# Soft mixture of experts by block sums on one core: ScalarE in program order, the first weight piece in two transfers, some z made later, the last round's stores on another queue

## The chip, the core and the metric

The kernel runs on one core of a Trainium2 chip. A core has five engines, each with its own instruction queue: TensorE (PE in the profile) multiplies matrices, VectorE (DVE) and ScalarE (ACT) work on elements and empty PSUM, GpSimd (POOL) and SyncE (SP) issue DMA transfers here. Weights, activations and intermediate blocks lie in SBUF; the results of matmuls lie in PSUM, which has eight banks of 128 x 512 float32 numbers. The metric is the device time of one execution, in microseconds (us).

## The reference

```python
batch, seq, hidden, n_experts, expert_hidden = 16, 512, 512, 8, 2048
...
probs = softmax(router_logits)               # over the 8 experts
for e in range(n_experts):
    expert_out = np.matmul(x, expert_weights[e])
    output += probs[:, :, e:e+1] * expert_out
```

(The softmax is written out there as exp of the logits less their maximum, divided by its sum.) There are 8192 rows of x. For one row, the output is a single long product: the row times each of its eight probabilities, all eight side by side (8 x 512 = 4096 numbers), times the eight weight matrices on top of each other (4096 x 2048). The kernel calls the left factor z.

## The kernel before

The long product is done in halves: two halves of the 8 experts (4 each), two halves of the 2048 columns, and 256-row blocks of x taken in pairs. On this 2 x 2 x 2 structure a Strassen-Winograd scheme is used, seven block products in place of eight, made of sums of z blocks, sums of weight blocks and sums of result blocks. The names a11, s1 to s4, t1 to t4, m1 to m7 in the code are those of that scheme. Inside most block products the same scheme is used once more. Matmuls take float16 operands and add up in float32.

The stages, in order of time:

1. *The start* (lines 196 to 439). `cast_x` and `cast_w` load x rows and weight pieces on GpSimd's queue, with a cast to float16; a weight piece is one expert's 512 rows by 512 columns, 512 KB in SBUF, and two pieces fill one `w` tile. The softmax of the first rows is computed, and the z of rows 0 to 511 is made by TensorE itself: x times a diagonal matrix of probabilities (`diag`, `early_z0`), evacuated from PSUM to SBUF by VectorE and ScalarE in turn (`evacuate`). Then the first product is made plainly, for two column halves n: four experts, four groups j of 128 rows, four chunks c of 128 hidden numbers, with one PSUM bank for each j (loop at 415 to 438). Four ScalarE copies (L432) empty those banks, and SyncE stores them. Behind each column half, `early_z1` makes the z of two of the groups j = 4 to 7 (rows 512 to 1023 of this order), 16 matmuls of 256 columns a time, two matmuls to a bank, for the next stage. The weight sums of the inner scheme (`inner_weights`, four VectorE instructions on a whole `w` tile each) are made between the two halves.
2. *Four stages of inner Strassen products* (`sub_product`, called for r = 1, 5, 2 and 4). Each result block goes to DRAM: `kept1`, `kept5`, `kept2`, and for r = 4 straight into the output. A generator (`prep`) loads and sums the next stage's weights meanwhile.
3. *The last stage* (line 578 on), 16 rounds q, each for one pair of row blocks. A round works on four quarters (row group t, column half n). For each quarter it loads the kept blocks m1, m5 and m2 (`load_kept`, `c11`); ScalarE copies m1 from SBUF into a PSUM bank (L604), and TensorE adds 16 matmuls to it (`plain` with w6). Such a copy into a bank that matmuls are then added to is called a *seed* here. VectorE reads the bank plus m5 into v, TensorE adds another 16 matmuls (w7) into the same bank, ScalarE copies it out (c21, L620), GpSimd adds it to the output in DRAM, VectorE sums it with m5 once more. Then, in round 0, four plain products with w3 follow, seeded with v (L637); in the later rounds an inner Strassen product of seven (`prod`): number 1 is copied to r1 (L666), number 2 is added to a bank seeded with v00 (L653), number 7 leaves a bank that ScalarE copies to r3 (L677) and that VectorE then sums in `put(2, ...)`; number 4 goes to a bank seeded with -v10, and its sum with r3 (`o10`) is made at the start of the next round.

VectorE prepares the z blocks of the next round between these sums (`a11`, `s2`, `s3`, `s4`, called by `ahead`); `early` loads the next round's first kept blocks and makes m1 + m2 (`c11`) and has GpSimd store it.

What sets the order. The program is written as one stream, and a scheduler places each instruction in its engine's queue from its own estimate of times, among those that it takes to be ready. `tc.keep_in_program_order(i)` ties an instruction behind the one traced before it on its engine. The helper `dve` does this for every VectorE instruction while `pinned[0]` is set, which it is in the start and in the last stage:

```python
    def dve(i):
        note(i)
        if pinned[0]:
            tc.keep_in_program_order(i)
```

ScalarE's copies have no such tie in the kernel before: `nc.scalar.copy(x, rows.m1[tn])` at L604 can stand in ScalarE's queue ahead of the copies that the text has before it. An engine takes its queue in order, so an instruction that waits holds all behind it. A tile's buffer is used again when its last reader is done (`m` has 5 buffers, `v` 4, `u` 4, `r` 2 in the last stage); PSUM's eight banks go round the same way.

Of the kernel before, what the change touches and what calls it, by code (L numbers as in the profile page):

```python
# [32 lines left out]
def kernel(  # L33
# [77 lines left out]
    def note(i):  # L111
        last[i.ins.engine] = i.ins

    def dve(i):
        note(i)
        if pinned[0]:
            tc.keep_in_program_order(i)

    def tt(o, a, b, op):
        dve(nc.vector.tensor_tensor(out=o, in0=a, in1=b, op=op))  # L120

# [11 lines left out]
    def pool(o, i):  # L133
        note(nc.gpsimd.dma_start(out=o, in_=i))  # L134

    def bank():
        return psum.tile([P, NB], f32, name="ps", tag="ps")

    def mm(ps, z, w, start, stop):
        nc.tensor.matmul(ps, z, w, start=start, stop=stop, skip_group_check=True)  # L140
# [5 lines left out]
    def new_w():  # L146
        return wpool.tile([P, K8, NB], f16, name="w", tag="w")

    def cast_w(q, kn, e, t):
        k, n = kn  # L150
        pool(t[:, ds(e * C, C), :],
             expert_weights[(q // 10 - 1) * HE + 2 * k + e, :,
                            ds((q % 10 - 1) * NH + n * NB, NB)].rearrange("(c p) n -> p c n", p=P))

    def load(what, kn, gate=True):
        t = new_w()
# [10 lines left out]
        stored[what, kn] = d = dram.tile([P, K8, NB], f16, name=f"wd{what}_{kn[0]}{kn[1]}")  # L167
        sp(d, t)

    def inner_weights(b, t3=None):  # L170
        t1 = new_w()
        tt(t1, b[0, 1], b[0, 0], SUB)
        yield
        t2 = new_w()
        tt(t2, b[1, 1], t1, SUB)
        t4 = new_w()
        tt(t4, t2, b[1, 0], SUB)
        yield
        t3 = t3 or b[0, 1]
        tt(t3, b[1, 1], b[0, 1], SUB)  # L180
        return {1: b[0, 0], 2: b[1, 0], 3: b[1, 1], 4: t4, 5: t1, 6: t2, 7: t3}


    def softmax(lg, J):
# [33 lines left out]
    with behind():  # L218
        for kn in BLOCKS[:3]:
            for e in range(2):  # L220
                cast_w(11, kn, e, b11[kn])
    cast_x(4)
    cast_x(6)
    for e in range(2):
# [13 lines left out]

    def evacuate(o, ps, i):
        if i % 2:  # L240
            note(nc.scalar.copy(o, ps))  # L241
        else:
            dve(nc.vector.tensor_copy(o, ps))  # L243

# [17 lines left out]
    def diag_j(j):  # L262
        return diag(ph0[1][:, :, ds(j % 4, 1)])

    def early_z1(j, d):
        for k in range(2):
            for c in range(0, C, 2):
                ps = bank()
                for i in range(2):
                    mm(ps[:, ds(i * 2 * P, 2 * P)], xs0[:, j, ds((c + i) * P, P)],  # L270
                       d[:, ds(2 * k, 2)].rearrange("p e t -> p (e t)"), i == 0, i == 1)
                evacuate(z1[j // 2 - 2][k][:, :, ds(c, 2), ds(j % 2 * P, P)],
                         ps.rearrange("p (c e t) -> p e c t", c=2, e=2), c // 2)


    R = 4
# [66 lines left out]
        sp(t, kept[r][i][n, ds(u * P, P), :])  # L343
        return t

    def sub_product(r, odd, first, w, prep, start=0, zs=None):

        for d in range(start, NI // 2):
            if zs:
# [13 lines left out]
            s2 = new(s1, a11, SUB)  # L363
            s4 = new(a12, s2, SUB)
            tt(a21, a11, a21, SUB)
            z = {1: a11, 2: a12, 3: s4, 4: a22, 5: s1, 6: s2, 7: a21}

            for u in range(HQ // P):
# [46 lines left out]
    for n in range(2):  # L415
        ps = [bank() for _ in range(4)]
        for e in range(HE):
            if n == 0 and e < HE - 1:
                if e < 2:
                    ds_.append(diag_e(e + 2))  # L420
                early_z0(e + 1, ds_[e + 1])
            for j in range(4):
                for c in range(C):
                    mm(ps[j], z0[j][:, e, c], b11[e // 2, n][:, e % 2 * C + c, :],
                       e + c == 0, e == HE - 1 and c == C - 1)
        if n == 0:
            ph0.append(early_p(1))
            ds_ = [diag_j(j) for j in range(4, 6)]
            softmax_of_all()
        for j in range(4):  # L430
            o = half()
            nc.scalar.copy(o, ps[j])  # L432
            to_kept(1, j // 2, j % 2, n, o)
        for i in range(2):
            early_z1(4 + 2 * n + i, ds_[i])
        if n == 0:
            ds_ = [diag_j(j) for j in range(6, 8)]
            with behind():
                w = finish(inner_weights(b11, new_w()))

    def weights_of_t1():
        b = {}
        for i, kn in enumerate(BLOCKS):
# [6 lines left out]
    pinned[0] = False  # L450
    share(xs=3, r=4, o=8)
    sub_product(1, 0, P1, w, weights_of_t1(), 1,
                [[z.rearrange("p e c t -> p (e c) t") for z in zz] for zz in z1])


    def weights_of_21():
# [50 lines left out]
    class Rows:  # L507
# [55 lines left out]
            self.put(0, 0, tn, m2)  # L563

        def put(self, odd, cols, tn, o, **how):
            nc.gpsimd.dma_start(out=out_rows(self.q, odd, tn[0], cols, tn[1]), in_=o, **how)  # L566

    rows = Rows(0)
    for make in (rows.a11, rows.s2, rows.s3):
# [8 lines left out]
    for q in range(NI):  # L578
# [11 lines left out]


        xs, vs = [], []
        if o10:
            o10()
        for j, tn in enumerate(QUARTERS):
            if j > 1:
                rows.load_kept(j)
                rows.c11(j)
            if j < 2:
                rows.s4(j)  # L600
            else:
                ahead("a11", j - 2)
            x = bank()
            nc.scalar.copy(x, rows.m1[tn])  # L604
            plain(x, 6, w6, tn, False)
            v = half("u")
            tt(v, x, rows.m5[tn], ADD)
            xs.append(x)
            vs.append(v)


        if q == 1:
# [3 lines left out]
        for j, tn in enumerate(QUARTERS):  # L616
            x, m5 = xs[j], rows.m5[tn]
            plain(x, 7, w7, tn, False)
            c21 = half("m")
            nc.scalar.copy(c21, x)  # L620
            rows.put(1, 0, tn, c21, accum_op=ADD)
            tt(m5, x, m5, ADD)
            rows.put(1, 1, tn, m5)
            if j < 2:
                ahead("s2", j)


        def early(j):
            if following:
                following.load_kept(j)  # L630
                following.c11(j)

        ahead("s3", 0)
        if q == 0:
            for j, tn in enumerate(QUARTERS):
                y = bank()
                nc.scalar.copy(y, vs[j])  # L637
                plain(y, 3, w3, tn, False)
                nc.scalar.copy(vs[j], y)
                rows.put(0, 1, tn, vs[j])  # L640
                if j < 2:
                    early(j)
                    next(sums)
            ahead("s3", 1)
            rows = following
            continue
        banks = {}

        def prod(p, b, seed=None, scale=1.0):
            if b not in banks:  # L650
                banks[b] = bank()
                if seed is not None:
                    nc.scalar.mul(banks[b], seed, scale)  # L653
            for k in range(K8):
                mm(banks[b], z3[p][:, k, :], inner3[p][:, k, :],
                   p in (1, 5) and k == 0, k == K8 - 1)
            return banks[b]
# [5 lines left out]
        v00, v01, v11, v10 = vs  # L663
        x = prod(1, "x")
        r1 = half("r")
        nc.scalar.copy(r1, x)  # L666
        put(0, prod(2, "b", v00), r1, ADD)
        early(0)
        r5 = prod(5, "q")
        tt(v11, r5, v11, ADD)  # L670
# [3 lines left out]
        put(1, prod(3, "q"), v01, ADD)  # L674
        prod(7, "x")
        r3 = half("r")
        nc.scalar.copy(r3, x)  # L677
        put(2, x, v11, ADD)
        ahead("s3", 1)
        d = prod(4, "d", v10, -1.0)  # L680

        def o10(put=put, r3=r3, d=d):
            put(3, r3, d, SUB)
# [30 lines left out]
```

## Time and profile before

| | us |
|---|---|
| median of 3 runs (lowest to highest) | 1446.75 (1442.5 to 1447.27) |
| the profiled execution's own time | 1446.23 |
| its span, first to last instruction | 1444.5 |
| TensorE busy | 1427.5 (99%) |
| VectorE busy | 1021.1 (71%) |
| ScalarE busy | 270.8 (19%) |
| GpSimd busy | 228.8 (16%) |
| granted TensorE clock | 0.998 of full speed |

The profile is of one execution. A line such as "L120 DVE TENSOR_TENSOR h<-ps,h" is an instruction of VectorE, written at line 120 (here a helper, `tt`), that reads the tiles ps and h and writes an h. In a timeline, the bracket at the end tells how long the engine stood idle before the first instruction of the line and what ended the wait. "PE" is a matmul, "PEld" the load of its stationary operand. Matmuls overlap in their pipeline, and their ends are modelled, so the length of one (379 ns in the mean) is longer than the step from one to the next. DMA transfers that a queue issues are listed with the queue (SPq, POOLq) and their time from issue to landing.

### The profile page before, as it was taken

To read this page: it belongs to the slowest core of one execution; us is meant where nothing else is said; L and a number is where in the kernel's file an instruction comes from. 1 tells how busy PE (TensorE), PEld (TensorE's weight loads), DVE (VectorE), ACT (ScalarE), POOL (GpSimd) and SP (SyncE) were. 2 spreads that over 40 slices of the span, in tenths; PEclk is the share of its full clock that TensorE was granted. 3 is DMA by queue.
4 is the path that set the end of the run, shared out by engine and by line. 5 is a ranking of instruction groups with operands and counts; after the bars stand their busy time and mean duration, and the time that the engine had idled before them with its cause. 6 is when DMAs were issued, how large, how long until landed. Compare 5 with 4: busy or idle time off the path is not lost.

```text
span 1444.5 us, 18192 instructions
## 1 busy us (share of the span) xinstructions
PE 1427.5 (99%) x6661; PEld 649.3 (45%) x6661; DVE 1021.1 (71%) x1171; ACT 270.8 (19%) x475; POOL 228.8 (16%) x357
## 2 busy tenths in 40 slices
PE   8999999999999999999999999999999999999997
PEld 4444444444444444444444444444444444444443
DVE  6857686747686867766757496777778787776774
ACT  3211111111111111111112111111111111111111
POOL 3100100110001000001000122222222222222222
PEclk9999999999999999999999999999999999999999
DMA  9989968899839994368866976787787777777773
GB/s 192 206 199 258 263 175 188 191 243 272 216 134 310 348 354 151 131 190 225 212 248 221 277 203 207 228 232 233 234 232 221 211 216 223 218 231 218 226 204 102
DMA packets 194073, 319.44 MB, mean 221 GB/s; under 512 B 54080, under 2 KB 83776, under 8 KB 189376
## 3 DMA queue, kind: packets, MB, share of 16 engines
q1 hardware_dynamic: 135616, 199.77, 44.8%
q0 software_dynamic: 58368, 118.51, 34.2%
q8 instruction: 52, 0.85, 0.2%
q14 instruction: 37, 0.30, 0.1%
HBM read 180.65 MB, written 159.58 MB: 236 GB/s over the span
## 4 chain that ended last, share of the span: by engine, by line
PE 52%; issue 34%; POOL 11%; DMA 1%; DVE 1%; POOLq 0%; ACT 0%; DVEq 0%; SPq 0%
PE ps L140 52%; POOL out_dram L566 11%; DMA w<-in_expert_weights_dram 1%; DVE h L120 0%; POOLq L566 0%; POOL w L134 0%; DMA out_dram<-h 0%; DMA h<-kept 0%; DVE z L120 0%; DVE z L243 0%; ACT h L432 0%; DVE h L190 0%; DVE h L191 0%; DVE h L186 0%; ACT h L188 0%
## 5 line engine op out<-in xcount | busy, mean ns | idle before, releaser
L140 PE MATMUL ps<-w,z 128*128 128x512 f16 x6552 | 1415.7, 379 | 5.2 <-DVE h L120 3.3
L140 PEld LDWEIGHTS <-z 128*128 128x128 f16 x6552 | 640.8, 98 | 778.3 <-issue 5.0
L120 DVE TENSOR_TENSOR h<-ps,h 128x512 f32<-128x512 f32 x389 | 265.7, 686 | 266.6 <-PE ps L140 65.8
L120 DVE TENSOR_TENSOR z<-xT,pT 128x2048 f16<-128x2048 f16 x248 | 299.3, 1218 | 31.9 <-PE ps L140 31.9
L120 DVE TENSOR_TENSOR z<-z 128x2048 f16<-128x2048 f16 x280 | 303.6, 1107 | 7.8 <-DVE z L120 0.5
L380 ACT COPY h<-ps 128x512 f32<-128x512 f32 x248 | 145.4, 586 | 601.6 <-PE ps L140 598.3
L566 POOL DMA_DIRECT2D out_dram<-h x256 | 162.1, 660 | 540.6 <-DVE h L120 499.9
L120 DVE TENSOR_TENSOR h<-h 128x512 f32<-128x512 f32 (+1 forms) x67 | 46.0, 686 | 78.7 <-DMA h<-kept 78.6
L620 ACT COPY h<-ps 128x512 f32<-128x512 f32 x64 | 37.5, 586 | 294.3 <-PE ps L140 208.6
L120 DVE TENSOR_TENSOR w<-w 128x4096 f16<-128x4096 f16 x36 | 82.2, 2286 | 3.3 <-DMA w<-wdt 2.0
L604 ACT COPY ps<-h 128x512 f32<-128x512 f32 x64 | 37.5, 588 | 197.9 <-DMA h<-kept 197.9
L134 POOL DMA_DIRECT2D h<-in_x_dram x32 | 22.5, 703 | 283.8 <-DMA xT<-h 249.9
L120 DVE TENSOR_TENSOR h<-h,ps 128x512 f32<-128x512 f32 x77 | 52.5, 682 | 11.6 <-PE ps L140 11.3
L134 POOL DMA_DIRECT2D w<-in_expert_weights_dram x40 | 29.9, 759 | 173.3 <-issue 77.3
L134 POOL DMA_DIRECT2D w<-wd x12 | 6.5, 543 | 188.3 <-DVE w L158 115.2
L653 ACT ACTIVATE ps<-h 128x512 f32<-128x512 f32 x30 | 18.2, 607 | 0.0
L243 DVE CAST z<-ps 128x512 f16<-128x512 f32 x16 | 10.2, 684 | 10.5 <-PE ps L140 10.5
L666 ACT COPY h<-ps 128x512 f32<-128x512 f32 x15 | 8.8, 586 | 16.4 <-PE ps L140 16.4
L241 ACT CAST z<-ps 128x512 f16<-128x512 f32 x16 | 8.4, 601 | 11.9 <-PE ps L140 11.9
L140 PE MATMUL ps<-h,w 128*128 128x128 f16 (+1 forms) x96 | 8.2, 237 | 2.3 <-DMA w<-in_x_dram 1.0
L677 ACT COPY h<-ps 128x512 f32<-128x512 f32 x15 | 8.7, 580 | 7.6 <-PE ps L140 7.6
L140 PEld LDWEIGHTS <-w 128*128 128x128 f16 x96 | 6.9, 98 | 4.3 <-DMA w<-in_x_dram 2.2
(31 smaller groups left out, 38.3 us busy)
## 6 DMA issues: line engine op xcount, KB each, us to landing
out_dram<-h POOLq DMA_DIRECT2D x256, 256.0 KB, 4.6
kept<-h SPq DMA_DIRECT2D x192, 256.0 KB, 4.7
h<-kept SPq DMA_DIRECT2D x192, 256.0 KB, 4.3
pT<-p_dram SPq DMA_DIRECT2D x124, 256.0 KB, 4.8
w<-in_expert_weights_dram POOLq DMA_DIRECT2D x40, 512.0 KB, 12.4
out_dram<-h SPq DMA_DIRECT2D x64, 256.0 KB, 3.7
xT<-x SPq DMA_DIRECT2D x60, 256.0 KB, 2.8
w<-wd POOLq DMA_DIRECT2D x12, 1024.0 KB, 9.4
```

Of the source, the lines that this page charges most:

```text
L120: dve(nc.vector.tensor_tensor(out=o, in0=a, in1=b, op=op))
L134: note(nc.gpsimd.dma_start(out=o, in_=i))
L140: nc.tensor.matmul(ps, z, w, start=start, stop=stop, skip_group_check=True)
L241: note(nc.scalar.copy(o, ps))
L243: dve(nc.vector.tensor_copy(o, ps))
L380: nc.scalar.copy(t, ps)
L566: nc.gpsimd.dma_start(out=out_rows(self.q, odd, tn[0], cols, tn[1]), in_=o, **how)
L604: nc.scalar.copy(x, rows.m1[tn])
L620: nc.scalar.copy(c21, x)
L653: nc.scalar.mul(banks[b], seed, scale)
L666: nc.scalar.copy(r1, x)
L677: nc.scalar.copy(r3, x)
```

## The change

- A second helper, `act`, is the same function as `dve`. The ScalarE copies of `evacuate`, of the first product's banks and of the whole last stage go through it, so they stay in program order in the start and in the last stage.
- In the last stage the seed of a quarter's bank now stands ahead of `o10` and of the quarter's `c11` in the text; the seeds of the banks "b" and "d" (in round 0 those of the first two w3 products) are written right behind the four w6 products, and the other two of round 0 behind the first two w3 products. The fourth copy and store of round 0 moves to the next round's `o10`. `c11` of round 1's first two quarters moves from round 0 into round 1.
- `cast_w` can load one expert's piece in two transfers of 256 KB (hidden chunks 0 and 1, then 2 and 3); this is used for the very first piece. In the first product the chunk loop c is now outside the group loop j.
- `early_z1` takes one (j, k) at a time, 8 matmuls, and all eight calls move into the second column half's product: two behind expert 0, three behind expert 1, three behind expert 2. The inner weight sums (`inner_sums` returns them as four callables) are made one behind expert 1, one behind the product, and two inside the first `sub_product`, after its z sums.
- In the last round (q = 15) the stores to the output that do not accumulate are issued by SyncE in place of GpSimd.

```diff
+    act = dve
...
-    def cast_w(q, kn, e, t):
+    def cast_w(q, kn, e, t, parts=1):
         k, n = kn
-        pool(t[:, ds(e * C, C), :],
-             expert_weights[(q // 10 - 1) * HE + 2 * k + e, :,
-                            ds((q % 10 - 1) * NH + n * NB, NB)].rearrange("(c p) n -> p c n", p=P))
+        for c in range(0, C, C // parts):
+            pool(t[:, ds(e * C + c, C // parts), :],
+                 expert_weights[(q // 10 - 1) * HE + 2 * k + e, ds(c * P, C * P // parts),
+                                ds((q % 10 - 1) * NH + n * NB, NB)].rearrange("(c p) n -> p c n", p=P))
...
+    def inner_sums(b, t3=None):
+        t3 = t3 or b[0, 1]
+        w = {1: b[0, 0], 2: b[1, 0], 3: b[1, 1], 7: t3}
+
+        def step(p, x, y):
+            if p not in w:
+                w[p] = new_w()
+            tt(w[p], x, y, SUB)
+        return w, [lambda: step(5, b[0, 1], b[0, 0]), lambda: step(6, b[1, 1], w[5]),
+                   lambda: step(4, w[6], b[1, 0]), lambda: step(7, b[1, 1], b[0, 1])]
...
-                cast_w(11, kn, e, b11[kn])
+                cast_w(11, kn, e, b11[kn], 2 if kn == (0, 0) and e == 0 else 1)
...
         if i % 2:
-            note(nc.scalar.copy(o, ps))
+            act(nc.scalar.copy(o, ps))
...
-    def early_z1(j, d):
-        for k in range(2):
-            for c in range(0, C, 2):
+    def early_z1(j, k, d):
+        for c in range(0, C, 2):
...
             s4 = new(a12, s2, SUB)
             tt(a21, a11, a21, SUB)
+            for make in rest:
+                make()
+            rest = ()
...
-            for j in range(4):
-                for c in range(C):
+            for c in range(C):
+                for j in range(4):
                     mm(ps[j], z0[j][:, e, c], b11[e // 2, n][:, e % 2 * C + c, :],
                        e + c == 0, e == HE - 1 and c == C - 1)
+            if n == 1:
+                for j, k in pieces[(0, 2, 5, 8)[e]:(2, 5, 8, 8)[e]]:
+                    early_z1(j, k, ds_[j - 4])
+                if e == 1:
+                    sums[0]()
+        for j in range(4):
+            o = half()
+            act(nc.scalar.copy(o, ps[j]))
+            to_kept(1, j // 2, j % 2, n, o)
         if n == 0:
             ph0.append(early_p(1))
-            ds_ = [diag_j(j) for j in range(4, 6)]
             softmax_of_all()
...
+            ds_ = [diag_j(j) for j in range(4, 8)]
+            pieces = [(j, k) for j in range(4, 8) for k in range(2)]
+            w, sums = inner_sums(b11, new_w())
+    sums[1]()
...
-            nc.gpsimd.dma_start(out=out_rows(self.q, odd, tn[0], cols, tn[1]), in_=o, **how)
+            queue = nc.sync if self.q == NI - 1 and not how else nc.gpsimd
+            queue.dma_start(out=out_rows(self.q, odd, tn[0], cols, tn[1]), in_=o, **how)
...
-        if o10:
-            o10()
         for j, tn in enumerate(QUARTERS):
             if j > 1:
                 rows.load_kept(j)
+            x = bank()
+            act(nc.scalar.copy(x, rows.m1[tn]))
+            if o10 and j == 0:
+                o10()
+            if j > 1 or q == 1:
                 rows.c11(j)
             if j < 2:
                 rows.s4(j)
             else:
                 ahead("a11", j - 2)
-            x = bank()
-            nc.scalar.copy(x, rows.m1[tn])
             plain(x, 6, w6, tn, False)
...
+        def seeded(b, v, scale=1.0):
+            banks[b] = bank()
+            act(nc.scalar.mul(banks[b], v, scale))
+        if q:
+            seeded("b", vs[0])
+            seeded("d", vs[3], -1.0)
+        else:
+            seeded(0, vs[0])
+            seeded(1, vs[1])
...
-            nc.scalar.copy(c21, x)
+            act(nc.scalar.copy(c21, x))
...
                 following.load_kept(j)
-                following.c11(j)
+                if q:
+                    following.c11(j)
...
-        nc.scalar.copy(r3, x)
+        act(nc.scalar.copy(r3, x))
```

## The prediction

> **What bounds the kernel now.** I read the page's engine shares first: TensorE is busy 1427.5 of 1444.5 us. The matmul group there has a mean of 379 ns, but that is a modelled, overlapped length. The timeline of TensorE shows the true pace: 1104 matmuls in 238.44 us, 216 ns each. At that pace the 6552 products alone take 1415 us, so only what lies before, between and behind them can be won. I therefore listed every break in the timeline of TensorE, first 0 to 30 us, then from 739 us to the end. Columns: start, length, engine, line, operation, operands, count, and in brackets the idle time before it with its releaser.
>
> ```profile
> 11.41 3.61 PE L140 MATMUL ps<-w,z 128*128 128x512 f16 x16 [1.79 <-DMA w<-in_expert_weights_dram]
> ...
> 27.00 1.47 PE L140 MATMUL ps<-h,w 128*128 128x256 f16 x12
> 29.23 0.60 PE L140 MATMUL ps<-h,w 128*128 128x256 f16 x4 [0.75 <-DVE z L243]
> ```
>
> ```profile
> 891.16 20.88 PE L140 MATMUL ps<-w,z 128*128 128x512 f16 x96 [1.21 <-DVE h L120]
> 912.85 238.44 PE L140 MATMUL ps<-w,z 128*128 128x512 f16 x1104 [0.81 <-DVE h L120]
> 1151.57 178.01 PE L140 MATMUL ps<-w,z 128*128 128x512 f16 x824 [0.28 <-DVE h L120]
> 1329.81 20.88 PE L140 MATMUL ps<-w,z 128*128 128x512 f16 x96 [0.23 <-DVE h L120]
> 1351.50 84.77 PE L140 MATMUL ps<-w,z 128*128 128x512 f16 x392 [0.81 <-DVE h L120]
> ```
>
> The first product waits 1.79 us for the first weight piece. The z of rows 512 to 767 takes 27.00 to 29.89, 2.89 us; the same 16 matmuls for rows 768 to 1023 take 43.70 to 45.44, 1.74. Then nothing until 890 us, and five gaps in the last stage, all ended by a VectorE sum. TensorE ends at 1436.27, the span 8.2 us later.
>
> Why VectorE is late there shows in the timelines of ScalarE and of VectorE, 876 to 885 us, just ahead of the first of the five:
>
> ```profile
> 883.29 0.59 ACT L604 COPY ps<-h 128x512 f32<-128x512 f32 x1 [3.85 <-DMA h<-kept]
> 883.82 0.58 ACT L677 COPY h<-ps 128x512 f32<-128x512 f32 x1
> ```
>
> ```profile
> 876.98 0.69 DVE L120 TENSOR_TENSOR h<-h 128x512 f32<-128x512 f32 x1 [5.30 <-DMA h<-kept]
> 877.59 0.68 DVE L120 TENSOR_TENSOR h<-ps,h 128x512 f32<-128x512 f32 x1
> 884.43 0.69 DVE L120 TENSOR_TENSOR h<-ps,h 128x512 f32<-128x512 f32 x1 [6.16 <-ACT h L677]
> ```
>
> The copy of r3 (L677) has its product since about 874, but stands behind a seed (L604) that waits for a kept block; VectorE stands 6.16 us. In the table of waits "DVE h L120 <- ACT h L677" is 58.6 us in 15 times. From 884.43 to 913 VectorE shows no idle time; at 891.16 TensorE wants a bank whose sum VectorE reaches 11 us after its product, and at 912.85 VectorE is still catching up.
>
> The tail is in the instructions of the program's end (L709): count, duration in ns min/median/max, first and last start.
>
> ```profile
> L709 POOLq DRAIN  x3: 51/102/6117, 1437.3 to 1443.9; - x3
> L709 SPq DRAIN  x3: 7/7/7, 1440.4 to 1443.6; - x3
> ```
>
> The last store is issued by GpSimd at 1437.29. SyncE has seen all landings by 1440.4, but GpSimd's drain, 6.12 us from 1437.3, ends at 1443.4, and the program's end follows 1.0 us later.
>
> [...]
>
> **The change part by part**, against the profiled execution: span 1444.5, its own time 1446.23, the median of the three runs 1446.75.
>
> *First piece in halves.* Before the gap TensorE stops at 9.62. The piece lands at 11.27 (issue 3.25 plus 8.02 in the chain of waits), with the DMA engines full and moving about 200 GB/s, so its second 256 KB take 1.3 us and the first half is there at about 10.0: 1.4 us won (bounds: 0 if the halves land together, 1.8 if z is the limit). The chunk-outer order needs the second half after 8 matmuls, 1.7 us later, at 11.7, when it has landed. The extra issue on GpSimd (0.75 us, from the x rows of 256 KB) delays the issues behind it, which queue for the full engines anyway; the next piece lands at 13.8 and is wanted at 10.0 + 3.45 + 0.89 = 14.3. Without that cover it would cost up to 0.75.
>
> *z of rows 512 to 1023 between products.* Removes 2.89 - 1.74 = 1.15 us. Adds: behind experts 1 and 2 six PSUM banks are wanted while four are free (eight less four accumulators). The fifth waits for the first evacuation, 0.42 after its matmuls start plus 0.68, at 1.1 instead of 0.88: 0.25 us each, 0.5 in all. Net 0.6, bounds 0 and 1.15. The weight sums move on VectorE: before 4 x 2.28 us at 32 to 41; now one among the z, one behind them and two behind the first four z sums (4 x 1.22). Counted from the z's end that is 2.3 + 4.9 + 4.6 = 11.8 us, done at about 52; the last of them is wanted by the seventh product, 6 x 1.73 us after a start at 43.4, so at 53.8. Hidden, with 1.7 us to spare. The four block copies (0.59 each) come together at each column half's end; four other banks are free.
>
> *ScalarE in program order.* r3 follows its product and the next round's first seed comes behind it. This takes the 3.9 us per round (58.6 / 15) off VectorE's queue, and 6.1 us before 891.16, which covers the 1.21, and, VectorE having been busy since, the 0.81 at 912.85; the other three are the same two places in later rounds. A gap's loss is its idle time plus 0.16, since idle counts from the modelled end (379 against 216): 3.34 + 5 x 0.16 = 4.1 us. I take 3.7, bounds 4.1 and minus what the next rival prices. The cost: the seed of a round's first product is today over 9 us early (at 907.91 for a product at 918). Now it runs in one product, 8 x 0.216 = 1.73 us: semaphore 0.25, r3 0.59, seed 0.53 behind it, 1.4. It fits with 0.3 us. Seeds b and d, early now, queue ahead of the round's first c21 copy; d waits for the fourth sum, which VectorE without its lag makes about 1 us behind its product, over 2 us before that copy can start; were it later, the c21 copies and the sums of their banks would slip with it. Two sums of round 0 move to round 1, 0.69 each, where VectorE has time.
>
> *Last stores on SyncE.* Twelve stores of the last round leave GpSimd. Its last transfer is then the accumulating one, about 1425 to 1426, and its drain is over by 1432. The end: VectorE's last sum ends at 1437.0, SyncE issues 0.1 later, the store lands after 2.3 (shortest of SyncE's 64 stores to the output; their median under load is 3.7, the shortest from GpSimd 2.6), SyncE's waits take 0.6 and the end 1.0: 1441.0, 3.4 us won. With the median landing it is 2.0; with a drain that still ends last, 0. The stores of round 15's first two sums now stand in SyncE's queue ahead of loads that feed seeds at 1401.44 for products at 1406.75: 5.3 us of cover.
>
> Sum: 1.4 + 0.6 + 3.7 + 3.4 = 9.1 us. 1446.75 - 9.1 = 1437.6.
>
> **Rivals.** *The seed becomes the wait (slower).* If r3 and the next seed take over 1.73 us, by a late bank or a kept block that lands late, TensorE stops once a round. The other parts bring 5.4, and VectorE's gaps are replaced: it turns slower than before when each of 15 rounds loses 0.36 us, at 2.1 us from product to seed, and leaves the 0.3% beyond 0.65. At 0.8 a round: 1446.75 - 5.4 + 12 = 1453. For it: 0.3 us of margin, and ScalarE's waits for kept blocks (197.9 us in 46 times). Against: a round's first block is there some 10 us ahead (the seed at 907.91 used it).
>
> *The gaps of the last stage stay.* VectorE also stands 5 to 6 us a round for kept blocks (876.98), and the change does nothing about that load. Then 5.4 us: 1441.4. Against: the lag at 891.16 is 1.2 us and 6.1 are taken away.
>
> *The tail stays.* GpSimd's drain may not depend on its last store, or stores to the output may land in 4 us behind other traffic. Then 5.7 to 7: 1440 to 1441; together with the rival before, 1444.7. Against: the drains of TensorE and VectorE end with those engines' last work, at 1436.3 and 1437.0. For it: GpSimd's goes on 5.6 us beyond its last issue, which this trace doesn't explain.
>
> *The halves do nothing:* they land together; 1.4 less, 1439.
>
> **How the numbers follow.** 0.3% is 4.3 us, about what a measurement here can tell from no change: under 1442.4 is faster, over 1451.1 slower. All or nearly all parts work (with or without the halves), 1435 to 1440: 0.60. One of gaps and tail stays, 1440 to 1442.4: 0.16. Both stay, or a new wait eats most: 1442.4 to 1451: 0.12. The seed's wait, or another the order brings: 0.12. Range 1434.5 to 1443.5: the first two cases and a little of the third; below 1446.75 - (1.8 + 1.15 + 4.1 + 3.4) = 1436.3 no bound reaches, and what is under it is for the runs' own scatter (1442.5 to 1447.27).
>
> **What would show it.** First product at about 10.0, sub-products from about 43.4 instead of 45.44; the r3 copy within 0.3 us of its product and no idle time of VectorE behind it; no TensorE gap from 800 us on; GpSimd's drain over before SyncE's, and the span 4.8 us behind the last matmul. I am wrong if TensorE shows a gap at the head of each round released by the seed, if sub-products start with gaps released by weight sums, or if the drain still ends at the end.

## The result, and the profile after

The changed kernel takes 1436.66 us (median of six runs, 1436.33 to 1436.9); the kernel before, run beside it, 1447.01 (six runs, 1442.5 to 1455.19). The ratio is 0.9926, 95% interval 0.9899 to 0.9953. The prediction was 1437.6, from 1434.5 to 1443.5. The profiled execution took 1436.33, its span 1434.5 (before: 1446.23 and 1444.5), with a granted clock of 1.0. So the spans differ by 10.0 us (9.94 in the finer times below); the prediction's sum was 9.1.

I cut both spans at the same four events: the first product, the first sub-product matmul, the end of the last matmul, the end.

| us | before | after | difference | predicted |
|---|---|---|---|---|
| start to first product | 11.41 | 10.84 | -0.57 | -1.4 |
| first product to first sub-product | 34.03 | 33.05 | -0.98 | -0.6 |
| first sub-product to last matmul's end | 1390.82 | 1386.67 | -4.15 | -3.7 |
| last matmul's end to end of span | 8.20 | 3.96 | -4.24 | -3.4 |

The start, in the timeline of TensorE of the changed kernel (columns as before):

```profile
10.84 3.61 PE L142 MATMUL ps<-w,z 128*128 128x512 f16 x16 [1.93 <-DMA w<-in_expert_weights_dram]
...
34.22 1.04 PE L142 MATMUL ps<-h,w 128*128 128x256 f16 x8
35.09 0.38 PE L142 MATMUL ps<-w,z 128*128 128x512 f16 x1
35.38 0.60 PE L142 MATMUL ps<-h,w 128*128 128x256 f16 x4
35.82 3.40 PE L142 MATMUL ps<-w,z 128*128 128x512 f16 x15
```

The first product still waits for the first weight transfer, now 1.93 us. The idle 0.75 us that stood at 29.23 before is gone. At the place where the fifth bank is not yet free, the scheduler slid one product matmul in (35.09); it took 0.29 us to the next start in place of 0.22.

The last stage, in the timeline of TensorE from 700 us to the end:

```profile
699.80 730.76 PE L142 MATMUL ps<-w,z 128*128 128x512 f16 x3385
```

One unbroken piece, where the kernel before had five gaps. Why, in the timelines of ScalarE and of VectorE at the same place of round 1 as the lines shown of before:

```profile
872.89 0.58 ACT L710 COPY h<-ps 128x512 f32<-128x512 f32 x1 [8.05 <-PE ps L142]
873.37 1.63 ACT L614 COPY ps<-h 128x512 f32<-128x512 f32 x3
```

```profile
871.41 0.69 DVE L122 TENSOR_TENSOR h<-h 128x512 f32<-128x512 f32 x1 [1.29 <-DMA h<-kept]
872.02 0.68 DVE L122 TENSOR_TENSOR h<-ps,h 128x512 f32<-128x512 f32 x1
873.50 0.69 DVE L122 TENSOR_TENSOR h<-ps,h 128x512 f32<-128x512 f32 x1 [0.80 <-ACT h L710]
```

The r3 copy (L710) is now released by its own product, and the sum that reads its bank follows after 0.80 us where it stood 6.16. (That sum does not read r3, yet it starts 0.03 us behind the copy's end: 884.40 and 884.43 before, 873.47 and 873.50 here.) Behind r3 come the seeds of the round's first three quarters. The first seed runs from 873.37 to 873.97; its product starts at 874.41, 0.44 us later. That is the margin that the prediction put at 0.3; of its 1.4 us, the 0.25 from the product's last step to the r3 copy is 0.20 here (872.69 to 872.89), and the 1.12 for r3 and the seed is 1.08 (to 873.97). The same margin stands at the head of every round from 2 to 15. The other wait of VectorE there, for a kept block (871.41), fell too, from 5.30 to 1.29 us, though I had said that the change does nothing about it. In the table of waits (us in all, times, longest):

```profile
ACT ps L614 <- DMA h<-kept: 38.0, 14, 7.6
...
DVE h L122 <- DMA h<-kept: 22.4, 13, 5.4
...
DVE h L122 <- ACT h L710: 18.7, 14, 1.7
```

Before, the first was 197.9 us in 46 times, the second 79.8 in 18, the third 58.6 in 15.

The end, in the instructions of the program's end (L742 here):

```profile
L742 POOLq DRAIN  x3: 51/102/7550, 1419.4 to 1434.2; - x3
L742 SPq DRAIN  x3: 7/7/7, 1433.7 to 1434.0; - x3
```

GpSimd's drain starts at 1419.4, lasts 7.55 us and is over at 1427, before TensorE is done. SyncE's last store is issued at 1431.32 and lands at 1433.60; that landing now sets the end, 0.9 us later.

### The profile page after: what moved, and what is told of

Its sections match the earlier page's. It is cut to its first block, busy times and chain, and to the rows that moved or that the text cites. A ratio compares the mean times of both kernels' runs of the same rounds, so it can differ in the third digit from the quotient of the medians.

```text
span 1434.5 us, 18198 instructions
## 1 busy us (share of the span) xinstructions
PE 1426.7 (99%) x6661; PEld 649.3 (45%) x6661; DVE 1030.2 (72%) x1171; ACT 272.7 (19%) x475; POOL 221.3 (15%) x346
## 4 chain that ended last, share of the span: by engine, by line
PE 99%; DMA 1%; POOL 0%; issue 0%; DVE 0%; POOLq 0%
PE ps L142 99%; DMA w<-in_expert_weights_dram 1%; POOL w L136 0%; DVE h L122 0%; POOL ident L227 0%; POOLq L227 0%; POOLq L731 0%
## 5 line engine op out<-in xcount | busy, mean ns | idle before, releaser
L583 POOL DMA_DIRECT2D out_dram<-h x244 | 153.6, 664 | 533.5 <-DVE h L122 324.0
L710 ACT COPY h<-ps 128x512 f32<-128x512 f32 x15 | 8.8, 585 | 120.7 <-PE ps L142 120.7
```

What stands on the lines that cost most here:

```text
L583: queue.dma_start(out=out_rows(self.q, odd, tn[0], cols, tn[1]), in_=o, **how)
L710: act(nc.scalar.copy(r3, x))
```

## The experiments

All landmarks in one table, each from that run's own profiled execution; "gaps" are the stops of TensorE behind the first sub-product, with the time lost in them; "slow" is what matmuls right behind a stop lost because the granted clock was one half for 3.4 us. "First" is the first product, "sub" the first sub-product. The time is the median of six runs (changed), nine (b_act), 20 (b_sp) and five (a_lg2), and a single run in the other rows. Beside them the kernel before took 1447.01 (median, beside the changed kernel), 1447.13 (median, beside the four parts), 1447.56 (median, beside a_lg2), and in single runs 1447.19 (beside b_pin, a_free, a_seed3 and a_lastpool) and 1444.63 (beside b_lastsp, a_lg and a_quarter).

| kernel | first | first to sub | sub to last matmul | gaps, lost | tail | span | time |
|---|---|---|---|---|---|---|---|
| before | 11.41 | 34.03 | 1390.82 | 5, 4.16 | 8.20 | 1444.5 | |
| changed | 10.84 | 33.05 | 1386.67 | 0 | 3.96 | 1434.5 | 1436.66 |
| before + ScalarE part (b_act) | 11.45 | 34.04 | 1386.91 | 1, 0.23 | 8.18 | 1440.6 | 1442.51 |
| before + SyncE stores (b_sp) | 10.94 | 34.03 | 1390.85 | 2, 2.50; slow 1.68 | 3.97 | 1439.8 | 1442.01 |
| before + halves (b_half) | 11.04 | 33.98 | 1390.66 | 5, 4.0 | 8.19 | 1443.9 | 1445.56 |
| before + z between products (b_z1) | 11.02 | 33.04 | 1391.77 | 6, 5.11 | 8.21 | 1444.0 | 1445.83 |
| before + ties alone (b_pin) | 10.69 | 34.04 | 1423.99 | 35, 37.42 | 8.27 | 1477.0 | 1478.79 |
| changed, no ties (a_free) | 9.83 | 33.04 | 1393.37 | 2, 5.19; slow 1.50 | 3.96 | 1440.2 | 1441.9 |
| changed, first seed three times (a_seed3) | 11.03 | 33.04 | 1398.46 | 14, 11.83 | 3.96 | 1446.5 | 1448.37 |
| changed, last store on GpSimd (a_lastpool) | 9.99 | 33.05 | 1386.67 | 0 | 7.53 | 1437.2 | 1439.12 |
| before, last store on SyncE (b_lastsp) | 10.96 | 34.04 | 1389.76 | 3, 3.1 | 6.84 | 1441.6 | 1443.59 |
| changed, logits later (a_lg) | 9.93 | 33.05 | 1387.19 | 1, 0.52 | 3.96 | 1434.1 | 1435.94 |
| the same again (a_lg2) | 10.36 | 33.14 | 1386.68 | 0 | 3.96 | 1434.1 | 1435.79 |
| changed, four transfers (a_quarter) | 10.92 | 34.73 | 1386.67 | 0 | 3.96 | 1436.3 | 1438.16 |

### Each part alone

The theory of the prediction: four independent parts, and the large ones are ScalarE's order and the drain. The rival: one part makes the room for another, so that alone it gives less or nothing. The four edits are the parts of the change's diff; their cores:

```diff
# b_act: the last stage alone
+            act(nc.scalar.copy(x, rows.m1[tn]))
+            if o10 and j == 0:
+                o10()
# b_sp
+            queue = nc.sync if self.q == NI - 1 and not how else nc.gpsimd
# b_half
+                cast_w(11, kn, e, b11[kn], 2 if kn == (0, 0) and e == 0 else 1)
# b_z1: with the weight sums in their new places and the ties of the start
+                for j, k in pieces[(0, 2, 5, 8)[e]:(2, 5, 8, 8)[e]]:
+                    early_z1(j, k, ds_[j - 4])
```

> The kernel before with only the last stage's ScalarE ties and moved seeds. Theory (the five TensorE gaps come from VectorE waiting behind a seed for r3's copy): no TensorE gap after the first product stage, last matmul 4.1 us earlier (about 1432.1), start and tail as before, span about 1440.4. Rival (the gaps come from VectorE's waits for kept blocks): gaps stay, span 1444. Rival (the seed becomes the wait): a gap at each round's head.

> The kernel before with only the last round's plain stores on SyncE. Theory (GpSimd's drain behind its last store held the end): 8.2 us behind the last matmul become about 4.0, span about 1440.2, gaps as before. Rival (only the store's landing gets shorter, 2.57 to 2.29): 0.3 us.

> The kernel before with only the first piece in two halves and the chunk loop outside. The prediction had the first product 1.4 us earlier (about 10.0); after the whole change it stood at 10.84, 0.57 earlier. If the half is held by the slowest of the 16 DMA engines, as it seems there (its landings ran from 9.24 to 10.71), 10.6 to 10.9 here too. If that was chance, about 10.0.

> The kernel before with only the z of rows 512 to 1023 (and its ScalarE ties and weight sums) moved between the products. Theory: from the first product to the first sub-product 34.03 us become about 33.05, as in the changed kernel; first product where it was. Rival: the moved weight sums or evacuations make gaps, and it stays at 33.5 or over.

Measured: the ScalarE part alone gives 1442.51 us against 1447.13 (median of the runs of the kernel before beside it), ratio 0.9972 (0.9958 to 0.9986); the SyncE stores alone 1442.01, ratio 0.9969 (0.9958 to 0.9981). The other two, one run each, came out at 1445.56 and 1445.83. In spans the four are 3.9, 4.7, 0.6 and 0.5 us below the kernel before: 9.7 together, where the whole change is 10.0. They add up, within what single executions scatter; no part needs another. The ScalarE part also took most of the scatter between runs: its nine runs lie within 2.8 us and the six of the changed kernel within 0.6, where the 20 of the SyncE stores spread over 9.3 us and the 28 of the kernel before over 8.7.

With the ScalarE part alone, the timeline of TensorE and two lines of the table of waits:

```profile
699.68 732.72 PE L142 MATMUL ps<-w,z 128*128 128x512 f16 x3393
```

```profile
DVE h L122 <- DMA h<-kept: 21.3, 16, 5.3
DVE h L122 <- ACT h L695: 19.4, 15, 1.7
```

The gaps are gone but for one of 0.23 us, and both waits of VectorE have fallen as in the changed kernel. So the shorter wait for kept blocks comes from this part as well. As both fell together, this run doesn't tell which of the two made the gaps, and the rival that names kept blocks is not excluded by it. (In the lines of before, the wait for r3 is the later of the two.) The part with z between products shows its 0.99 us where it was expected, from first product to first sub-product, and gave back as much in the last stage, where its execution lost 5.11 us in gaps in place of 4.16. That loss differs between kernels that share one last stage (4.18 with the SyncE stores, 4.0 with the halves, 3.1 with the last store alone on SyncE); gains of the start under a microsecond can't be read from whole times as long as the gaps are there.

### Ties without the moved seeds, moved seeds without the ties

What does the ScalarE part consist of? One theory: the ties alone free VectorE, and moving the seeds is ornament. A second: the text's new order alone is enough for the scheduler. Mine: both are needed, since tied in the old text the seed would stand behind work that waits.

```diff
# b_pin, against the kernel before: every ScalarE copy of the last stage so, none moved
-            nc.scalar.copy(x, rows.m1[tn])
+            act(nc.scalar.copy(x, rows.m1[tn]))
# a_free, against the changed kernel
-    act = dve
+    act = note
```

> The kernel before with the last stage's ScalarE copies tied to program order, and no seed moved in the text. Theory (a tied queue makes each seed wait for the copy before it): the seeds of banks b and d now stand right behind the r1 and r3 copies, done about 1.4 us behind the product whose successor needs them, so TensorE stops about 1.4 us twice in each of 15 rounds: about 40 us slower, 1484. Rival (the ties alone are what helps): 1440.

> The changed kernel with its ScalarE copies not tied, the seeds where the changed text has them. If the ties are what keeps the r3 copy ahead of the seeds: the r3 copy waits for seeds again, TensorE gaps return, 2 to 5 us slower than the changed kernel (span 1437 to 1440). If the new place in the text is enough: span 1434.5.

Measured: ties alone 1478.79 us, 31.6 above the kernel before run beside it (1447.19). From its table of waits and its timeline of TensorE:

```profile
PE ps L142 <- ACT ps L655: 25.6, 30, 1.2
...
PE ps L142 <- ACT ps L639: 4.9, 4, 1.2
```

```profile
873.13 8.15 PE L142 MATMUL ps<-w,z 128*128 128x512 f16 x37 [0.53 <-ACT ps L655]
882.45 31.89 PE L142 MATMUL ps<-w,z 128*128 128x512 f16 x147 [1.18 <-ACT ps L655]
914.87 8.15 PE L142 MATMUL ps<-w,z 128*128 128x512 f16 x37 [0.53 <-ACT ps L655]
```

L655 is the seed of banks b and d. Tied where the old text has them, they are made when their product is due: TensorE stops for each of them, twice a round, in all 15 rounds, four times in round 0 for the w3 seeds (L639), and once for a quarter's seed. The two stops of a round lose 0.69 and 1.34 us, where 1.4 each was expected. VectorE's wait for r3 is short here (22.6 us in 15 times), and it helps nothing.

The new text without ties lost 6.69 us. (The edit drops the ties of the start too, but from first product to first sub-product nothing changed.) The scheduler put r3 behind a waiting seed again; the timeline of ScalarE:

```profile
881.98 0.59 ACT L614 COPY ps<-h 128x512 f32<-128x512 f32 x1 [1.95 <-DMA h<-kept]
882.51 0.58 ACT L710 COPY h<-ps 128x512 f32<-128x512 f32 x1
```

The product of this r3 had ended at 878.08. In rounds 1 to 14 the r3 copy starts 4.4 to 8.0 us behind its product here and 5.6 to 9.4 in the kernel before, but 0.04 in every round of the changed kernel, of b_act and of b_pin: keeping r3 behind its own product is the work of the ties. VectorE's wait for the r3 copy is 56.8 us in 15 times without them, much as before the change. Yet TensorE stopped only once for VectorE, at 1272.05, and lost 0.45 us. The rest has another releaser, in the timeline of TensorE:

```profile
848.79 3.40 PE L142 MATMUL ps<-w,z 128*128 128x512 f16 x8 [4.58 <-ACT ps L614]
```

Here a seed itself came late, that of round 1's fourth quarter: its kept block arrived at 848.07, after ScalarE had waited 11.59 us for it. The stop loses 4.58 + 0.16 = 4.7 of the 6.69 us, and the matmuls right behind it run at half clock, which loses another 1.5. Why the block was late shows in the timeline of ScalarE ahead of it:

```profile
834.47 0.59 ACT L614 COPY ps<-h 128x512 f32<-128x512 f32 x1 [10.31 <-DMA h<-kept]
835.00 1.55 ACT L667 COPY h<-ps 128x512 f32<-128x512 f32 x3
848.14 0.59 ACT L614 COPY ps<-h 128x512 f32<-128x512 f32 x1 [11.59 <-DMA h<-kept]
```

The copies of three w3 products of round 0 (L667), the first of them ready at about 827, stand behind a seed that waits until 834.47. GpSimd stands idle for 10.04 us until the first copy, then issues four stores at once, from 835.87 to 837.47, which take 6.7 to 6.9 us to land. SyncE's queue waits for one of them until 843.80 (at this place until 839.75 in the changed kernel), and the load of the late block stands behind that. So it is the same mechanism at another place, ready copies behind a waiting seed; this is read from one trace and was not tried apart. The changed kernel has little slack at this seed too: it ends at 844.71 for a product at 845.06, and coming late it cost 0.23 us in b_act and 0.52 in a_lg below.

The wait of VectorE for kept blocks is 74.1 us with the ties off, and 21.7 in the kernel with ties alone: the ties shorten that wait, not the moves. Whether it is by way of the late stores just described was not tried.

So the ties keep ready copies from standing behind a seed that waits, and the moves keep the tied seeds ahead of the products that want them. What stays open is how much of the five gaps of the kernel before came from the wait for r3 by itself. Without ties that wait remains, and VectorE still held TensorE up for only 0.45 us, in an execution in which a stop of 4.7 us had come first and may have given VectorE the time to catch up.

### How near the seed is to being the wait

The main rival of the prediction was that the first seed of a round becomes late. I lengthened it by two copies of the same block into the same bank:

```diff
-            act(nc.scalar.copy(x, rows.m1[tn]))
+            for _ in range(3 if q and j == 0 else 1):
+                act(nc.scalar.copy(x, rows.m1[tn]))
```

> The changed kernel with the first seed of each round from 1 to 15 written three times over, so two copies of 0.52 us more stand between the r3 copy and the product; the result is the same. Theory (that seed is done 0.44 us ahead of its product): TensorE stops 0.6 us at the head of 14 or 15 rounds, 8 to 9 us slower, span 1443. If more slack is in it: less, and no gap.

Timelines of TensorE and of ScalarE:

```profile
875.44 39.87 PE L142 MATMUL ps<-w,z 128*128 128x512 f16 x184 [0.68 <-ACT ps L615]
916.00 39.87 PE L142 MATMUL ps<-w,z 128*128 128x512 f16 x184 [0.68 <-ACT ps L615]
```

```profile
873.07 0.59 ACT L711 COPY h<-ps 128x512 f32<-128x512 f32 x1 [8.04 <-PE ps L142]
873.55 2.87 ACT L615 COPY ps<-h 128x512 f32<-128x512 f32 x5
```

TensorE stops at the head of rounds 2 to 15, 14 times, released by the seed (round 1 has no r3 ahead of its first seed); each stop loses 0.845 us, 11.83 in all, and the time is 1448.37. Five copies take 2.87 us where three took 1.63: 1.24 for the two, not the two steps of 0.52 that my expectation of 0.6 rested on. Copies into the same bank start 0.62 us apart, where one takes 0.59 to 0.60, so none starts before the one ahead of it has ended; those into different banks start 0.52 apart and overlap. 1.24 less the margin of 0.44 is 0.80, near the 0.845. So the rival's mechanism is real, its point of decision lies 0.44 us away, and past it each round pays.

### The end

Theory: GpSimd's drain ends last because of its late store. Rival: the drain doesn't depend on that store, and the gain comes from having fewer stores there. One store moved back, and one store moved alone:

```diff
# a_lastpool, against the changed kernel
+            last = odd == 0 and cols == 1 and tn == QUARTERS[3]
+            queue = nc.sync if self.q == NI - 1 and not how and not last else nc.gpsimd
# b_lastsp, against the kernel before
+            last = self.q == NI - 1 and odd == 0 and cols == 1 and tn == QUARTERS[3]
+            (nc.sync if last else nc.gpsimd).dma_start(out=..., in_=o, **how)
```

> The changed kernel with only its very last store back on GpSimd. Theory (GpSimd's drain lasts about 5.6 us beyond its last issue): the end moves 3.5 to 4.2 us out, span about 1438.5. Rival (only the landing counts): 0.3 to 0.6 us, span 1435.

> The kernel before with only its very last store on SyncE. Theory (drain 5.6 us beyond GpSimd's last issue, which is now 1.06 us earlier): the end comes 1.0 us earlier, 7.2 us behind the last matmul. Rival (the last store's landing sets the end): as with all plain stores moved, about 4 us behind the last matmul.

The ends of the two programs, the first with the last store back on GpSimd:

```profile
L743 POOLq DRAIN  x3: 51/102/5740, 1430.7 to 1437.0; - x3
L743 SPq DRAIN  x3: 7/7/7, 1433.9 to 1436.7; - x3
```

```profile
L710 POOLq DRAIN  x3: 51/102/6105, 1434.7 to 1441.3; - x3
L710 SPq DRAIN  x3: 7/7/7, 1438.3 to 1441.1; - x3
```

One store back on GpSimd makes the tail 7.53 us in place of 3.96. Its store lands at 1433.39, and the drain goes on to 1436.5. With only the very last store on SyncE the tail falls from 8.20 to 6.84, since GpSimd's second last store, issued at 1434.73, then starts the drain: 1430.7 to 1436.5 and 1434.7 to 1440.8 are 5.7 and 6.1 us. The drain follows the last store that GpSimd issues, whichever that is, while SyncE has seen the landings by 1433.9 and 1438.3, 2.6 and 2.5 us before its end. It ends 3.0 to 3.5 us behind that store's landing in all 14 traces: 3.5 in the six kernels that keep more than one late plain store on GpSimd, 3.1 in a_lastpool, and 3.0 in the seven that have none there. In those seven the last store is an early one, and the drain costs nothing. Why it goes on beyond the landing stays open.

### The first transfer

The halves gave 0.57 us where 1.4 was expected. The sixteen landings of the first half, one for each DMA engine, show where the time went: the earliest is at 9.24 us, half of them are there by 9.47, and the latest is at 10.71. The first product follows the sixteenth, 0.13 us after it (10.84), and 0.14 us in the kernel before (11.27 and 11.41). Two thoughts followed. If the four loads of all router logits, which SyncE issues in the same time, hold up the late engine, then issuing them later should bring the first product to about 10 us. If smaller transfers are better, four should beat two.

```diff
# a_lg, a_lg2, the same kernel (against the changed one; the call stands behind the first early_z0)
-    for r in range(R):
-        sp(lg_all[ds(r * NHQ, NHQ)], lg_v[r])
+    def load_all_logits():
+        dve(nc.vector.memset(lg_all[:, 0:1, 0:1], 0.0))
+        for r in range(R):
+            sp(lg_all[ds(r * NHQ, NHQ)], lg_v[r])
# a_quarter
-                cast_w(11, kn, e, b11[kn], 2 if kn == (0, 0) and e == 0 else 1)
+                cast_w(11, kn, e, b11[kn], 4 if kn == (0, 0) and e == 0 else 1)
```

> The changed kernel with SyncE's four loads of the full router logits (256 KB) held until VectorE has evacuated the first z, by a small memset of their tile. If these loads take the DMA engines from the first weight piece: it lands up to 1.3 us earlier and the first product starts at about 9.7 in place of 10.84, span 1433.4. If they don't matter: 10.8.

> The changed kernel with the logits' loads held, a second time and timed. Of the five earlier traces with the first piece in halves and the logits loaded early, two had the first product at 9.83 and 9.99 and three at 10.84 to 11.04; the one with the logits held had 9.93. If the logits' loads make the late ones: 9.9 again. If it is chance: as likely 10.8 to 11.1. The time: 1436 either way; at best 0.6 us under the changed kernel, which is less than the runs can tell.

> The changed kernel with the first weight piece in four transfers. A quarter is 128 KB, 0.65 us at 200 GB/s: if the piece's landing is what the first product waits for, it starts at 10.1 to 10.3, and each further quarter is there before its four matmuls (0.86 us a quarter against 0.65). If a late DMA engine holds any piece: 10.8, or a gap of some tenths behind the first four matmuls.

With the logits later the first product starts at 9.93 and 10.36 us. But the kernels with the halves and the logits where they were lie at 9.83, 9.99, 10.84, 11.03 and 11.04, those with the whole piece at 10.69, 10.94, 10.96, 11.02, 11.41 and 11.45. The means are 10.55 and 11.08, but the five with halves spread over 1.2 us, and three of them lie among the six others. So a gain from the halves is likely but not settled. The five timed runs with the logits later have the median 1435.79 (ratio 0.9918, 0.9904 to 0.9931), which overlaps with the changed kernel's 0.9926. So it isn't settled whether the logits matter.

With four transfers the first product starts at 10.92, the second case of the expectation: fifteen of the sixteen engines have their part of the first quarter in by 9.64 us, the last at 10.78. The run was also slower than the changed kernel, for a reason that I had not thought of. The timeline of TensorE, then the windows around it (us of the window, busy time of each engine, granted clock, DMA share, GB/s):

```profile
10.92 5.30 PE L142 MATMUL ps<-w,z 128*128 128x512 f16 x16 [2.01 <-DVE h L122]
```

```profile
10.90:12.60 1.70, 1.68 (x5) 0.69 (x6) 0.02 (x1) 0.00 (x0) 1.53 (x3) 0.57 1.25 208
12.60:14.40 1.80, 1.80 (x5) 0.61 (x4) 0.00 (x0) 0.00 (x0) 1.36 (x2) 0.50 1.24 205
14.40:16.00 1.60, 1.60 (x8) 0.72 (x7) 0.00 (x0) 0.00 (x0) 0.60 (x1) 0.95 1.25 207
```

(The bracket names a VectorE instruction that ended in the same moment; the landing at 10.78 lies 0.14 us ahead of the start.) The same 16 matmuls take 5.30 us in place of 3.61. No wait lies between them: the granted clock is 0.5 for 3.4 us, and they start 427 ns apart. TensorE had paused for 2.23 us, from one start to the next, ahead of them. The length of the pause does not decide: two other traces (b_z1 and a_seed3) have one of 2.23 and 2.32 us there and kept their clock. The cases differ in where the pause lies against the times at which the clock changed. In the trace of the kernel before the clock is full for 1433.598 us (from 4.769), which is 420 steps of 3.4133, and in that of the changed kernel for 1430.184 us (from 5.085), 419 such steps; in both it is halved only behind the last matmul. In all 14 traces every change of the granted clock lies a whole number of these steps behind the first record of full clock, and the busy time of TensorE within a step goes with the clock of the next:

| run and step, us | TensorE busy, us | clock in the next step |
|---|---|---|
| a_free, 845.05 to 848.47 | 0.00 | half |
| a_quarter, 7.74 to 11.15 | 1.40 | half |
| b_sp, 870.06 to 873.47 | 1.44 | half |
| changed, 8.50 to 11.91 | 1.48 | full |
| b_act, 7.59 to 11.00 | 1.51 | full |
| b_z1, 870.36 to 873.78 | 1.99 | full |

Up to the last matmul, every other step of the 14 traces has 1.6 us or more and is followed by full clock. So in these traces the clock was halved behind a step with 1.44 busy us of 3.41 or less, and not behind one with 1.48 or more (ends of matmuls are modelled, so the border is not known to some hundredths). Where the steps fall differs from run to run: the first begins at 4.17 us in one trace and at 7.09 in another. Four transfers did not lengthen the pause (2.01 us idle against 1.93 in the changed kernel), and the changed kernel's own start is only 0.04 us of busy time away from a case that was slow (b_sp). That four transfers bring the slow start about is therefore not shown.

## Why the prediction was right, and where it was off

*First piece in halves: mechanism partly right, size wrong.* The spacing held: the second 256 KB land 1.28 us behind the first (1.3 predicted), and 1.26 to 1.34 in the five traces with halves. The step that failed is the starting point of the sum, that the whole piece still lands at 11.27 when it is sent in two. It was in at 11.99, and so the first half was in at 10.71, not at about 10.0. In the five traces the split piece is complete at 11.03 to 12.18, the whole one in six at 10.55 to 11.31. In this trace the slowest engine came 1.2 us behind the eighth of the sixteen, in the kernel before 0.7 (10.54 and 11.27); why it is later with two transfers stays open. The term was -1.4, measured -0.57, where single executions with halves lie up to 1.2 us apart. The cover that the step named held: the second half, in at 11.99, was wanted at 10.84 + 8 x 0.216 = 12.57.

*Z between products: right, the stall mis-sized.* I priced the fifth bank at 0.25 us twice. The scheduler put a product matmul between, and the stall came to 0.07 twice; 1.15 - 0.14 = 1.01, measured 0.98. The weight sums went as worked out: the last one ends at 52.50 (predicted 52), and the seventh product starts at 43.89 + 6 x 1.73 = 54.3.

*ScalarE in program order: right.* The sum was 4.1 at most, taken as 3.7, and all of the gaps went: 4.15. The r3 copy came directly behind its product, the seed behind it with 0.44 us to spare, and the runs with ties alone and with a longer seed show that both of these links carry. That the wait for r3 by itself made the gaps is not shown: without the ties it stayed, and VectorE held TensorE up for 0.45 us. Wrong was a side remark: that VectorE's waits for kept blocks would stay. They fell from 79.8 to 22.4 us, and the runs without and with ties show that the ties do it. So VectorE had more taken off it than I worked out.

*Last stores on SyncE: mechanism right, size 0.8 too small.* The drain ended before TensorE, and the store landed in 2.28 us as taken (2.3). I then let SyncE's waits and the end take 0.6 and 1.0; they took 0.9 together, from 1433.60 to 1434.5. The last transfer of GpSimd was issued at 1419.43; with TensorE's end 5.7 us earlier, that is 1425.1 on the clock of the kernel before, as predicted (1425 to 1426).

The rivals: the seed did not become the wait, but would have with 0.44 us more; the gaps did not stay; the tail did not stay, and the run with one store back on GpSimd shows that it would have cost 3.57 us; whether the halves did more than chance is not settled. (For the tail that stays with landings in 4 us the prediction has a gain of 7; its own terms give 9.1 - 1.7 = 7.4.) The errors of the four terms are +0.8, -0.4, -0.45 and -0.8 us, -0.8 together: 9.1 was predicted and 9.9 measured. That the first and the last cancel is luck, and the sum came out nearer than its parts deserve.

## What to carry to other kernels

When an engine is late, look at what stands ahead of its producer in that producer's queue: here a copy whose data was ready stood behind a seed that waited for a load, and it took both a fixed order and an earlier place in the text to mend it; in one run each, the place without the order lost 6.7 us again, and the order without the place cost 31. Before a tie is set, list what the tied instruction feeds and how much slack it will have; here 0.44 us of it decides over 0.8 us per round. The end came 1.0 us behind GpSimd's drain in the kernel before and 0.9 behind SyncE's landing in the changed one: see which queue settles last. The last few plain stores belong on one that is done soon after its last landing, all of them and not only the very last: here the tail was 8.20 us with all on GpSimd, 7.53 with the very last on GpSimd, 6.84 with only the very last on SyncE, and 3.96 with all on SyncE.

## What the runs showed of the hardware

- GpSimd's drain at the program's end went on until 3.0 to 3.5 us beyond the landing of its last store, in all 14 traces and wherever that store stood; where the store was late this was 5.7 to 6.1 us beyond its start. In the changed kernel SyncE's store of the same size let the program end 0.9 us after landing (1433.60 and 1434.5).
- The first product started 0.13 to 0.14 us behind the last of the 16 landings, one for each DMA engine, of its first weight transfer. In the changed kernel's first half these came 1.5 us apart (9.24 to 10.71), in a_quarter's first quarter 2.7, with fifteen of them in by 9.64 us and the last at 10.78.
- The granted clock of TensorE changed, in the 14 traces, only at multiples of 3.413 us behind its first full record (419 of them in the changed kernel, 420 in the kernel before). Up to the last matmul it was halved for the next 3.4 us (427 ns a matmul) behind the three steps with 0.00, 1.40 and 1.44 us of busy TensorE, and behind none with 1.48 or more.
- Two more ScalarE copies into a PSUM bank that had just been written cost 1.24 us, 0.62 each (a_seed3: five copies in 2.87 us, against three in 1.63); copies into different banks followed each other after 0.52 (873.37, 873.89 and 874.41 in the changed kernel).
